# First projections of half 0 taken from x without 1/rms, with a fixed order up to the third feature tile

## The chip, the cores and the metric

The kernel runs on one core of one Trainium2 chip. The metric is the device time of one execution in microseconds. A core has TensorE (PE, with its weight loads shown as PEld), VectorE (DVE), ScalarE (ACT), GpSimd (POOL) and SyncE (SP, which here only issues DMAs). Each works through its own queue in order and waits on semaphores for the others.

## The reference, cut to what matters

One layer with 1024 positions and 1024 features; only its first step is touched by the change:

```python
def rmsnorm(x, g):
    y = x * lax.rsqrt(jnp.mean(x * x, axis=-1, keepdims=True) + EPS)
    return y * g

def swiglu(x, w_gate, w_up, w_down):
    return (jax.nn.silu(x @ w_gate) * (x @ w_up)) @ w_down

x = x + 0.5 * swiglu(rmsnorm(x, ffn1_norm), ffn1_w_gate, ffn1_w_up, ffn1_w_down)
x = x + hybrid_mixer(rmsnorm(x, mix_norm), ...)
x = x + 0.5 * swiglu(rmsnorm(x, ffn2_norm), ffn2_w_gate, ffn2_w_up, ffn2_w_down)
y = rmsnorm(x, final_norm)
```

Each position's row is multiplied by one number, its 1/rms, and each feature by its gain. As 1/rms belongs to a position, it can be put to the rows before a projection or to the projection's products after it.

## The kernel before

**Numbers.** TensorE multiplies in fp32r. To keep fp32 accuracy every operand is split into a high part (a cast on ACT, `S.copy`, L92) and a low part (source minus high part, on DVE, L85 by way of `sub`), and every product is three matmuls of 128 x 128 by 128 x 512: high by high, high by low, low by high (`PASSES`).

**Layout.** x is held with features on partitions, as 8 tiles of 128 features by 1024 positions; a *half* is 512 positions (`xh(k, n)`). The inner dimension of the feed-forward step, 2816, is cut into 22 feature tiles of 128. A product of 1024 features has eight inner steps: `q` is the half of the features (four steps each).

**Order of the work.** Tiles 0 and 1 are taken plainly (`plain`): half 0 of tile 0, half 0 of tile 1, half 1 of tile 0, half 1 of tile 1, with 48 matmuls each (gate and up, two banks of PSUM, 8 inner steps, 3 passes). From tile 2 on (`ups`) a tile's four blocks (gate and up by two halves) are taken together in Strassen's way, with seven products of 12 matmuls, in the order 1, 5, 6, 2, 7, 3, 4 (`UPS`), each of a left operand made from the weights (L11, T1, T2, L12, T3, L22, T4) and a right one made from x (R11, S1, S2, R21, S3, S4, R22). R11 and R21 are half 0, R12 and R22 half 1; S1 to S4 are sums and differences of these. After each second tile, `down` takes the pair through the down projection, 84 matmuls (L588).

**The start.** `Norm.add` squares a feature tile on ACT (L300) and adds it to a chain (L88) on the engine `chain`; `Norm.fin` sums over partitions with a tiny matmul (L318), takes the power -0.5 on POOL (L329), puts it on a diagonal (L333), spreads it over the partitions with another matmul (L337) and, if `keep`, copies it to SBUF (L341). `Norm.raw` (L345) makes x times gain times 1/rms on DVE. `half0` makes R11 and R21, `half1` makes R12, R22, S1 and S2 and POOL's subtractions (L85, hraw) for S3 and S4, `half1_end` S3 and S4. Half 0's chain is on DVE, half 1's on POOL. Half 0's 1/rms is left in PSUM, half 1's is copied to SBUF.

**Weights and queues.** `plan` and `plan_plain` put loads and splits in a list of steps; `pump` takes steps from its head as long as buffers are free, and `tick` calls it, counts planned time and resumes the generators given to `spawn`. All loads go through SP's queue. `pre` makes the operands of a pair's down projection.

**What fixes the order.** `in_order` chains all instructions of an engine in the order of the program; `behind` only puts later instructions behind the last one of that chain. Before, the order of TensorE, DVE, ACT and POOL is fixed up to the end of `half0`; after that TensorE alone is, and a scheduler places the others.

Of the kernel before, what the change touches and what calls it, by code (L numbers as in the profile page):

```python
# [16 lines left out]
P = 128  # L17
# [38 lines left out]
def trunk(ctx: ExitStack, tc: tile.TileContext, a, out):  # L56
# [22 lines left out]
    def t2(name):  # L79
        return room("t2", name)  # L80
# [36 lines left out]
    def pump(n=None):  # L117
        while todo and n != 0:
            n = n and n - 1
            tag, step = todo[0]  # L120
            if not tag():
                return
            todo.popleft()
            step()

    def free(tag, n=1):
        used[tag] -= n
        assert used[tag] >= 0
# [42 lines left out]
            if p == 6:  # L171
                sums(4)

    def load(st, src):
        def go(i):
            st[i] = room("wr", "raw")
            nc.sync.dma_start(out=st[i], in_=src[i])

        for i in range(2):
            todo.append((room_for("wr"), lambda i=i: go(i)))  # L180

    def plan_plain(key, src, order, home=None, when=None):
# [18 lines left out]
        load(st, src)  # L201
# [40 lines left out]
    def spawn(gen, wait=0.0):  # L242
        later.append([clock[0] + wait, gen])

    def tick(us):
        pump()
        clock[0] += us
        for e in list(later):
            if e[0] <= clock[0]:
                w = next(e[1], None)  # L250
                if w is None:
                    later.remove(e)
                else:
                    e[0] = clock[0] + w
# [9 lines left out]
    S.activation(warm, nhalf[:, 0:1], AF.Silu)  # L264
    ones = cp.tile([P, P], F32, name="ones")
    V.memset(ones, 1.0)
    ident = cp.tile([P, P], F32, name="ident")
# [4 lines left out]
    def xh(k, n):  # L272
        return xs[k][:, n * HALF:(n + 1) * HALF]
# [15 lines left out]
    class Norm:  # L289


        def __init__(self, c, w=HALF, chain=None):
            self.c, self.w, self.n, self.chain, self.sums = c, w, w // P, chain, []

        def x(self, k):
            return xs[k][:, self.c:self.c + self.w]

        def square(self, k):
            q = t2("sq")[:, :self.w]
            S.activation(q, self.x(k), AF.Square, scale=D ** -0.5)  # L300
            return q

# [17 lines left out]
        def fin(self, bank, keep=True, waits=(2.7, 1.3), fill=lambda: None):  # L320

            n = self.n
            st = bank("st")
            self.stat([st[:, 2 * j:2 * j + 2] for j in range(n)], self.sums[0], True, True)
            ss = tiny.tile([P, 8], F32, tag="st", name=nm("ss"))
            fill()
            V.tensor_scalar_add(ss[:, 0:2 * n], st[:, 0:2 * n], EPS)
            r = tiny.tile([P, 4], F32, tag="rs", name=nm("rs"))
            G.tensor_tensor(r[:, :n], ss.rearrange("p (j c) -> p j c", c=2)[:, :n, 0], nhalf[:, :n], op=ALU.pow)  # L329
            fill()  # L330
            yield waits[0]
            dg = t2("dg")[:, :self.w]
            V.tensor_tensor(dg.rearrange("p (j c) -> p j c", j=n), ident.unsqueeze(1).to_broadcast([P, n, P]),  # L333
                            r[:, :n].unsqueeze(2).to_broadcast([P, n, P]), op=ALU.mult)
            yield waits[1]
            rp = bank("rb")[:, :self.w]
            nc.tensor.matmul(rp, ones, dg, start=True, stop=True)  # L337
            self.r = rp
            if keep:
                self.r = t2("rb")[:, :self.w]  # L340
                S.copy(self.r, rp)  # L341
            fill()

# [16 lines left out]
    class Ffn:  # L360
        def __init__(self, i, g):
            self.i, self.g = i, g
            self.raws, self.h, self.acts, self.pool, self.start = {}, {}, {}, None, None


        def weights(self):
            w, wd = a[f"ffn{self.i}_w"], a[f"ffn{self.i}_wd"]
            by_k = ("L11", "L21", "L12", "L22")
            plan_plain((self.i, "f", 0), w[0], by_k)
# [86 lines left out]
        def plain(self):  # L456
            for n in range(2):
                for f in range(2):
                    pss = [self.bank(4 * n + 2 * f + m) for m in range(2)]
                    for q in range(2):  # L460
                        lts = [need(((self.i, "f", f), f"L{m + 1}{q + 1}")) for m in range(2)]
                        for k, rk in enumerate(self.r_of(f"R{q + 1}{n + 1}")):
                            for m in range(2):
                                for t, (i, j) in enumerate(PASSES):
                                    c = 512 * i + k * P
                                    nc.tensor.matmul(pss[m], lts[m][:, c:c + P], rk[j],
                                                     start=(q == 0 and k == 0 and t == 0),
                                                     stop=(q == 1 and k == 3 and t == 2))
# [9 lines left out]
                        tick(1.36)  # L478


        def ups(self, f, pre=None):
# [135 lines left out]

        def run(self, after, shut, ranges):
            since = here()
            self.plain()  # L620
            for _ in self.side:
                pass
            spawn(self.half1_end())
            if self.start:
                behind(self.start)
            for f in range(2, NF):
                g = f // 2 - 1
                if f % 2:
                    self.ups(f)
                else:  # L630
                    self.ups(f, lambda: self.pre(g))
                    self.down(g)
            shut()
            in_order(since, nc.tensor)
            self.end = here()
            self.down_last(after, ranges)
# [421 lines left out]
    side = lambda es, n: es.enter_context(tc.tile_pool(name=n, bufs=1, reuse_waits="tile"))  # L1058

    f1, f2 = Ffn(1, 0), Ffn(2, 2)  # L1060
    n1 = [Norm(0, chain=V), Norm(HALF, chain=G)]
    n2 = [Norm(0), Norm(HALF, chain=G)]
    n3 = [Norm(0), Norm(HALF)]
    tail = [(0, HALF), (HALF, 256), (HALF + 256, 256)]
# [6 lines left out]
    eh, ep = ExitStack(), ExitStack()  # L1071
    f1.pool = side(eh, "h1")
    f1.pp = psum(ep, "p1")
    for k in range(KT):
        nc.sync.dma_start(out=xh(k, 0), in_=a["x"][k * P:(k + 1) * P, 0:HALF])
    nc.sync.dma_start(out=gains, in_=a["gains"])
    nc.sync.dma_start(out=ident, in_=a["ident"])
    pump(2)
    for k in range(KT):
        n1[0].add(k)  # L1080
    begin = n1[0].fin(f1.bank_norm, False)
    next(begin)
    pump(2)
    next(begin)
    next(begin, None)
    pump(4)
    for k in range(KT):
        nc.sync.dma_start(out=xh(k, 1), in_=a["x"][k * P:(k + 1) * P, HALF:T])
    nc.sync.dma_start(out=w_a1, in_=a["w_a1"])
    for k, _ in enumerate(f1.half0(n1[0])):  # L1090
        if k >= 4:
            pump(1)
        n1[1].add(k)
    f1.start = in_order(0, nc.tensor, V, S, G)
# [6 lines left out]
    f1.side = second(f1, n1[1], 8.0)  # L1101
    spawn(f1.side)
    pump()
    hm = [[], []]

    def to_mix(n, d):
# [164 lines left out]
```

## Time and profile before

| | before |
|---|---|
| median of 3 runs | 1818.57 us (1815.8 to 1819.06) |
| the profiled execution's own time | 1820.42 us |
| its span, first to last instruction | 1818.6 us |
| PE busy | 1743.9 us, 96% |
| DVE busy | 1377.7 us, 76% |
| ACT busy | 830.1 us, 46% |
| POOL busy | 649.6 us, 36% |
| granted TensorE clock, mean | 0.981 |

The time of an execution is the span and 1.8 us around it. Busy time is added up over each engine's instructions. Matmuls overlap each other, so a busy TensorE is not one at its peak; the start times of matmuls show its pace. In rows of the timeline an "x8" stands for eight instructions in a row that were merged, with the time from the first's start to the last's end; the bracket names the idle time before them and what ended it.

### The profile page before, as it was taken

How to read it: one execution, taken by the hardware profiler on the slowest of the kernel's cores; microseconds unless marked ns; L12 is line 12 of the kernel's file. 1: busy time of each engine (PE TensorE's matmuls, PEld its weight loads, DVE VectorE, ACT ScalarE, POOL GpSimd, SP SyncE). 2: the span in 40 equal slices, each digit the busy share in tenths (PEclk: the TensorE clock that was granted, in tenths of full speed). 3: DMA queues.
4: the chain of work that ended last, by engine and by line, in shares of the span. 5: the costliest groups of instructions: out<-in, count | busy, mean ns of one | idle time of the engine just before them, and what ended most of it. 6: DMA issues, size and time to landing. Idle time of an engine off the chain costs nothing.

```text
span 1818.6 us, 20907 instructions
## 1 busy us (share of the span) xinstructions
PE 1743.9 (96%) x7774; PEld 1426.4 (78%) x7774; DVE 1377.7 (76%) x1825; ACT 830.1 (46%) x1439; POOL 649.6 (36%) x442
## 2 busy tenths in 40 slices
PE   5999999999999998899999999999999999999994
PEld 4788888888888875788888887888888888888883
DVE  6897778877798775765646668787788777887785
ACT  4445445554455444532352444454455544554443
POOL 3454254533444232220211021442545335442433
PEclk9999999999999998999999999999999999999997
DMA  5011212111111211222122222012121121112102
GB/s 188 24 47 47 70 47 67 49 47 59 58 46 47 70 53 46 70 92 81 62 90 90 82 72 96 21 35 70 47 70 47 46 66 50 47 48 69 58 13 93
DMA packets 35110, 112.92 MB, mean 62 GB/s; under 512 B 4384, under 2 KB 6848, under 8 KB 35008
## 3 DMA queue, kind: packets, MB, share of 16 engines
q1 hardware_dynamic: 33376, 109.48, 18.3%
q10 hardware_dynamic: 1632, 2.10, 0.3%
q8 instruction: 61, 1.00, 0.2%
q14 instruction: 41, 0.34, 0.1%
HBM read 107.37 MB, written 4.19 MB: 61 GB/s over the span
## 4 chain that ended last, share of the span: by engine, by line
PE 47%; issue 21%; POOL 18%; DVE 11%; ACT 2%; DMA 0%; POOLq 0%; SPq 0%; ACTq 0%; DVEq 0%
PE ps L588 16%; POOL x L88 12%; PE pj L702 12%; PE ps L354 5%; PE dn L1007 5%; POOL raw L85 4%; DVE S L85 2%; PE v L757 2%; DVE S L88 2%; POOL hraw L85 2%; PE ps L608 2%; PE sc L826 1%; DVE hraw L345 1%; DVE sq L88 1%; DVE T L85 1%
## 5 line engine op out<-in xcount | busy, mean ns | idle before, releaser
L354 PE MATMUL ps<-R,w 128*128 128x512 f32 x1920 | 455.5, 391 | 8.7 <-DVE act L88 8.6
L354 PEld LDWEIGHTS ps<-R,w 128*128 128x128 f32 x1920 | 359.3, 188 | 91.8 <-DVE act L88 17.1
L588 PE MATMUL ps<-act,w 128*128 128x512 f32 x1680 | 388.1, 391 | 0.0
L588 PEld LDWEIGHTS ps<-act,w 128*128 128x128 f32 x1680 | 313.8, 188 | 71.2 <-DVE act L512 6.5
L354 PE MATMUL ps<-S,w 128*128 128x512 f32 x1440 | 342.0, 391 | 3.0 <-ACT ps L493 3.0
L85 DVE TENSOR_TENSOR w<-raw,w 128x512 fp32r<-128x512 f32 x316 | 278.4, 887 | 77.3 <-ACT w L92 77.3
L354 PEld LDWEIGHTS ps<-S,w 128*128 128x128 f32 x1440 | 271.9, 189 | 60.0 <-ACT ps L493 3.4
L85 POOL TENSOR_TENSOR raw<-raw 128x512 f32<-128x512 f32 x60 | 78.5, 1309 | 612.7 <-DVE w L85 610.9
L92 ACT CAST w<-raw 128x512 fp32r<-128x512 f32 x316 | 195.3, 619 | 173.0 <-POOL raw L85 79.1
L88 POOL TENSOR_TENSOR x<-x,dx 128x512 f32<-128x512 f32 x160 | 266.5, 1702 | 17.3 <-ACT dx L575 17.3
L526 DVE SCALAR_TENSOR_TENSOR x<-ps,x 128x512 f32<-128x512 f32 x320 | 210.2, 683 | 35.5 <-PE ps L588 35.5
L702 PE MATMUL pj<-h,whi 128*128 128x512 f32 x640 | 200.5, 395 | 0.0
L85 DVE TENSOR_TENSOR wlo<-raw,whi 128x1024 fp32r<-128x1024 f32 x64 | 80.4, 1256 | 89.5 <-PE pj L702 47.7
L85 DVE TENSOR_TENSOR w<-T,w 128x512 fp32r<-128x512 f32 x120 | 118.1, 984 | 38.1 <-ACT w L92 38.1
L702 PEld LDWEIGHTS pj<-h,whi 128*128 128x128 f32 x640 | 119.0, 189 | 26.2 <-issue 1.9
L218 ACT CAST whi<-raw 128x1024 fp32r<-128x1024 f32 x64 | 67.0, 1047 | 139.1 <-PE pj L702 81.8
L702 PE MATMUL pj<-h,wlo 128*128 128x512 f32 x320 | 124.9, 390 | 0.0
L85 DVE TENSOR_TENSOR act<-act,act 128x512 fp32r<-128x512 f32 x98 | 105.3, 1076 | 13.6 <-ACT act L92 13.6
L92 ACT CAST w<-T 128x512 fp32r<-128x512 f32 x120 | 74.6, 622 | 54.3 <-PE ps L354 32.0
L85 POOL TENSOR_TENSOR raw<-raw,raw 128x512 f32<-128x512 f32 x60 | 97.3, 1622 | 4.6
L92 ACT CAST act<-act 128x512 fp32r<-128x512 f32 x98 | 60.8, 622 | 74.8 <-PE ps L588 44.2
L85 DVE TENSOR_TENSOR T<-raw,raw 128x512 f32<-128x512 f32 x60 | 48.7, 812 | 55.7 <-POOL raw L85 55.7
(170 smaller groups left out, 2133.3 us busy)
## 6 DMA issues: line engine op xcount, KB each, us to landing
raw<-in_ffn_w SPq DMA_DIRECT2D x88, 512.0 KB, 3.5
raw<-in_ffn_wd SPq DMA_DIRECT2D x44, 512.0 KB, 3.7
raw<-in_w_fm SPq DMA_DIRECT2D x40, 512.0 KB, 3.5
raw<-in_w_out SPq DMA_DIRECT2D x16, 512.0 KB, 3.5
x<-in_x SPq DMA_DIRECT2D x16, 256.0 KB, 6.3
raw<-in_w_v SPq DMA_DIRECT2D x8, 512.0 KB, 3.5
out<-y SPq DMA_DIRECT2D x2, 512.0 KB, 2.9
out<-y ACTq DMA_DIRECT2D x2, 512.0 KB, 2.8
```

The source lines that it names most:

```text
L85: eng.tensor_tensor(o, x, y, op=ALU.subtract)
L88: eng.tensor_tensor(o, x, y, op=ALU.add)
L92: S.copy(hi, src)
L218: S.copy(st[1], st[0])
L345: V.scalar_tensor_tensor(o, self.x(k), gains[:, g, k:k + 1], self.r, op0=ALU.mult, op1=ALU.mult)
L354: nc.tensor.matmul(ps, lt[:, c:c + P], rk[j], start=(start and n == 0), stop=(n == last), skip_group_check=True)
L526: V.scalar_tensor_tensor(xh(d, n), ps, 0.5, xh(d, n), op0=ALU.mult, op1=ALU.add)
L588: nc.tensor.matmul(ps, l2[i], r[0][j], start=(start and n == 0), stop=(n == 2), skip_group_check=True)
L608: nc.tensor.matmul(ps, l2[i], rts[h][q][:, 512 * j + o:512 * j + o + w], start=(q == 0 and k == 0), stop=(q == 1 and k == 2))
L702: nc.tensor.matmul(pss[f], w[i][:, k, f * P:(f + 1) * P], h[j][:, 4 * kh + k, :], start=(kh == 0 and k == 0 and n == 0), stop=(kh == 1 and ...
L757: nc.tensor.matmul(pss[t], h[i][:, kk, t * P:(t + 1) * P], u[j][:, k * 512:(k + 1) * 512], start=(kk == 0 and i == 0 and j == 0), stop=(kk ...
L1007: nc.tensor.matmul(pss[j], w[p][:, f * 512 + j * P:f * 512 + (j + 1) * P], act[q][i][:, f * 512:(f + 1) * 512], start=(i == 0 and f == 0 a ...
```

## The change

For half 0 of tiles 0 and 1 the right operands become x times gain (X11 and X21, split like the rest), with no 1/rms; the products of gate and up are multiplied by 1/rms afterwards, on DVE, ahead of Silu. Weights of tile 0 and the gains are loaded through ACT's queue, x through SP's; x of half 1 is loaded behind tile 1's weights. Half 0's chain of squares goes to POOL, half 1's to DVE. R11 and R21 are still needed from tile 2 on: ACT multiplies by the gain and POOL by 1/rms (`raw0`). The differences of x's halves are formed in another order: POOL takes r0 = raws0 - r0 and r1 = r1 - r0, and S1 = raws0 + r1. All buffers are assigned by hand. The order of TensorE, DVE, ACT and POOL is that of the program up to the end of tile 2's `ups`; `hold` stops `pump` in `tick` until `rest` has been through.

```diff
-            nc.sync.dma_start(out=st[i], in_=src[i])
+            queue.dma_start(out=st[i], in_=src[i])
...
     def tick(us):
-        pump()
+        if not hold:
+            pump()
...
+        def block(self, f, n, rights):
+            pss = [self.bank(4 * n + 2 * f + m) for m in range(2)]
+            for q in range(2):
+                lts = [need(((self.i, "f", f), f"L{m + 1}{q + 1}")) for m in range(2)]
+                for k, rk in enumerate(self.r_of(rights[q])):
+                    for m in range(2):
+                        for t, (i, j) in enumerate(PASSES):
...
+                    yield pss
...
+        def opening(self, n0, n1, load1):
+            T = [t2("op") for _ in range(14)]
...
+            def xpart(k):
+                t, g = h[("X11", "X21")[k // 4]], gains[:, self.g, k:k + 1]
+                S.mul(t[:, 0, k % 4, :], xh(k, 0), g)
+                V.scalar_tensor_tensor(t[:, 1, k % 4, :], xh(k, 0), g, t[:, 0, k % 4, :].bitcast(F32),
+                                       op0=ALU.mult, op1=ALU.subtract)
+
+            def raw0(i):
+                o = raws[divmod(i, 4)]
+                S.mul(o, xh(i, 0), gains[:, self.g, i:i + 1])
+                G.tensor_tensor(o, o, n0.r, op=ALU.mult)
...
+            pump(1)
+            xpart(0)
+            pump(1)
+            xpart(1)
+            for k in range(6):
+                n0.add(k)
+                xpart(k + 2)
+                if k in (1, 2):
+                    pump(1)
+            pump(2)
+            load1()
+            b = self.block(0, 0, ("X11", "X21"))
+            for ps00 in b:
+                pass
+            n0.add(6)
+            n0.add(7)
+            pump(4)
+            for k in range(5):
+                n1.add(k)
+            fin = n0.fin(self.bank_norm)
+            next(fin)
+            pump(2)
+            b = self.block(1, 0, ("X11", "X21"))
+            n1.add(5)
+            next(b), next(b)
+            next(fin)
+            n1.add(6)
+            n1.add(7)
+            next(b)
+            next(fin, None)
+            a00 = T[13]
+            V.tensor_tensor(a00, ps00[0], n0.r, op=ALU.mult)
+            V.tensor_tensor(ps00[1], ps00[1], n0.r, op=ALU.mult)
+            S.activation(a00, a00, AF.Silu)
+            raw0(0)
...
+            b = self.block(0, 1, ("R12", "R22"))
+            a10 = T[12]
+            row(0)
+            for i in range(8):
+                if i < 7:
+                    row(i + 1)
+                rowpart(i)
+                if i == 1:
+                    V.tensor_tensor(a10, ps10[0], n0.r, op=ALU.mult)
+                    V.tensor_tensor(ps10[1], ps10[1], n0.r, op=ALU.mult)
+                    S.activation(a10, a10, AF.Silu)
+                if i == 3:
+                    V.tensor_tensor(a10, a10, ps10[1], op=ALU.mult)
+                if i < 4:
+                    raw0(4 + i)
+                    sub(G, r[0, i], raws[0, i], r[0, i])
+                ps01 = next(b)
+            for _ in b:
+                pass
+            for k in range(4):
+                sub(G, r[1, k], r[1, k], r[0, k])
+            h["S3"] = h["X21"]
+            parts("S3", range(4), lambda k: r[0, k])
...
+            b = self.block(1, 1, ("R12", "R22"))
+            pump(2)
+            V.tensor_tensor(a01, a01, ps01[1], op=ALU.mult)
+            next(b), next(b)
+            parts("R11", range(4), lambda k: raws[0, k])
+            next(b), next(b)
+            h["S1"] = h["X11"]
+            for k in range(4):
+                add(V, raws[0, k], raws[0, k], r[1, k])
+                self.part("S1", k, raws[0, k])
+                if k == 1:
+                    pump(3)
...
+            def rest():
+                pump(1)
+                self.right("S2", "S3")
+                parts("S2", range(4), lambda k: r[1, k])
+                pump(2)
+                parts("R21", range(4), lambda k: raws[1, k])
+                yield 2.7
+                pump(1)
+                h["S4"] = h["R12"]
+                for k in range(4):
+                    sub(G, raws[1, k], raws[1, k], r[1, k])
+                for k in range(4):
+                    parts("S4", (k,), lambda k: raws[1, k])
+                    if k == 1:
+                        yield 2.7
+                raws.clear()
+                hold.clear()
...
-    n1 = [Norm(0, chain=V), Norm(HALF, chain=G)]
+    n1 = [Norm(0, chain=G), Norm(HALF, chain=V)]
```

In `run`, the opening takes the place of `plain` and `half1_end`, and the chain of `in_order` now ends behind `ups` of tile 2:

```diff
-                if f % 2:
+                if f == 2 and self.norms:
+                    self.ups(f, lambda: self.pre(g))
+                    start = in_order(0, nc.tensor, V, S, G)
+                    self.down(g)
+                    behind(start)
+                elif f % 2:
```

## Rows read from the trace of the kernel before

**Rows 1.** The page, busy time by engine and TensorE in 40 slices of the span.

```profile
PE 1743.9 (96%) x7774; PEld 1426.4 (78%) x7774; DVE 1377.7 (76%) x1825; ACT 830.1 (46%) x1439; POOL 649.6 (36%) x442
...
PE   5999999999999998899999999999999999999994
```

**Rows 2.** Timeline of TensorE: start us, length us, engine, line, operation, tiles.

```profile
20.56 10.08 PE L466 MATMUL ps<-R,w 128*128 128x512 f32 x31 [1.49 <-ACT R L92]
...
51.21 5.60 PE L466 MATMUL ps<-S,w 128*128 128x512 f32 x24
...
62.09 5.60 PE L466 MATMUL ps<-S,S 128*128 128x512 f32 x24
67.53 5.60 PE L466 MATMUL ps<-R,S 128*128 128x512 f32 x24
72.97 5.60 PE L354 MATMUL ps<-R,w 128*128 128x512 f32 x24
81.54 5.49 PE L354 MATMUL ps<-S,w 128*128 128x512 f32 x12 [2.96 <-ACT ps L493]
...
98.49 19.51 PE L588 MATMUL ps<-act,w 128*128 128x512 f32 x84
117.84 5.60 PE L354 MATMUL ps<-R,w 128*128 128x512 f32 x24
...
153.81 3.06 PE L354 MATMUL ps<-R,w 128*128 128x512 f32 x12 [0.45 <-DVE act L88]
```

**Rows 3.** Timeline and windows of the start: loads, first casts, DMA (last columns: share, GB/s).

```profile
0.72 1.28 ACT L264 ACT_TABLE_LOAD   x1 [0.72 <-PEq L1263]
7.27 2.38 SPq L177 DMA_DIRECT2D raw<-in_ffn_w  x4
12.18 2.42 ACT L92 CAST w<-raw 128x512 fp32r<-128x512 f32 x4 [0.86 <-DMA raw<-in_ffn_w]
...
0.00:5.38 5.38, 0.00 (x0) 0.00 (x0) 0.22 (x2) 2.74 (x4) 0.19 (x4) 1.00 0.58 171
5.38:20.56 15.18, 3.94 (x10) 2.28 (x11) 9.54 (x16) 6.72 (x12) 1.39 (x1) 1.00 0.99 365
```

**Rows 4.** Timeline: the sums over partitions and the spread of the second norm.

```profile
35.45 1.06 PE L318 MATMUL ps<-ones,sq 128*128 128x2 f32 x8 [0.31 <-POOL sq L88]
42.16 1.02 PE L337 MATMUL ps<-dg,ones 128*128 128x512 f32 x2
```

**Rows 5.** Timeline of DVE and POOL, each alone and both at work.

```profile
31.81 1.29 POOL L88 TENSOR_TENSOR sq<-sq,sq 128x512 f32<-128x512 f32 x1 [1.35 <-ACT sq L300]
44.51 4.72 DVE L345 SCALAR_TENSOR_TENSOR hraw<-x,gains,rb 128x512 f32<-128x512 f32 x7
51.55 2.50 DVE L85 TENSOR_TENSOR R<-hraw,R 128x512 fp32r<-128x512 f32 x4
60.15 4.69 POOL L85 TENSOR_TENSOR hraw<-hraw,hraw 128x512 f32<-128x512 f32 x1 [19.40 <-DVE hraw L85]
66.50 1.75 POOL L85 TENSOR_TENSOR hraw<-hraw,hraw 128x512 f32<-128x512 f32 x1
67.01 1.78 DVE L85 TENSOR_TENSOR w<-raw,w 128x512 fp32r<-128x512 f32 x1
68.21 3.44 POOL L85 TENSOR_TENSOR hraw<-hraw,hraw 128x512 f32<-128x512 f32 x2
68.72 3.48 DVE L85 TENSOR_TENSOR S<-hraw,S 128x512 fp32r<-128x512 f32 x2
1121.02 1.79 DVE L345 SCALAR_TENSOR_TENSOR hraw<-x,gains,rb 128x512 f32<-128x512 f32 x1
```

**Rows 6.** Windows: length, then busy (count) of PE, PEld, DVE, ACT, POOL; PEclk, DMA, GB/s.

```profile
51.20:72.97 21.77, 21.77 (x97) 18.02 (x96) 21.77 (x28) 8.62 (x16) 12.82 (x6) 1.00 0.08 25
72.97:98.49 25.52, 22.44 (x85) 17.66 (x84) 19.83 (x24) 10.88 (x20) 9.77 (x7) 0.87 0.07 21
81.50:86.80 5.30, 5.26 (x12) 4.12 (x13) 2.41 (x5) 1.53 (x3) 0.00 (x0) 0.50 0.32 99
```

More of the change, by code (lines that the diff above doesn't have):

```diff
@@ L172, in plan, with load, plan_plain @@
                 sums(4)
-    def load(st, src):
+    def load(st, src, queue=nc.sync):
         def go(i):
             st[i] = room("wr", "raw")
-            nc.sync.dma_start(out=st[i], in_=src[i])
+            queue.dma_start(out=st[i], in_=src[i])
         for i in range(2):
             todo.append((room_for("wr"), lambda i=i: go(i)))
-    def plan_plain(key, src, order, home=None, when=None):
+    def plan_plain(key, src, order, home=None, when=None, queue=nc.sync):
         st = {}
@@ L199, in part @@
             todo.append((when or room_for("wo"), go))
-        load(st, src)
+        load(st, src, queue)
         where = {"L11": (0, 0), "L12": (1, 1), "L21": (0, 1), "L22": (1, 0)}
@@ L243, in spawn @@
         later.append([clock[0] + wait, gen])
+    hold = []
     def tick(us):
-        pump()
+        if not hold:
+            pump()
         clock[0] += us
@@ L263, in trunk @@
     warm = cp.tile([P, 1], F32, name="warm")
-    S.activation(warm, nhalf[:, 0:1], AF.Silu)
     ones = cp.tile([P, P], F32, name="ones")
@@ L293, in __init__, with room @@
             self.c, self.w, self.n, self.chain, self.sums = c, w, w // P, chain, []
+            self.homes = {}
+        def room(self, s):
+            return self.homes[s] if s in self.homes else t2(s)[:, :self.w]
         def x(self, k):
@@ L298, in square @@
         def square(self, k):
-            q = t2("sq")[:, :self.w]
+            q = self.room(f"sq{k}" if self.homes else "sq")
             S.activation(q, self.x(k), AF.Square, scale=D ** -0.5)
@@ L331, in fin @@
             yield waits[0]
-            dg = t2("dg")[:, :self.w]
+            dg = self.room("dg")
             V.tensor_tensor(dg.rearrange("p (j c) -> p j c", j=n), ident.unsqueeze(1).to_broadcast([P, n, P]),
@@ L339, in fin @@
             if keep:
-                self.r = t2("rb")[:, :self.w]
+                self.r = self.room("rb")
                 S.copy(self.r, rp)
@@ L362, in __init__ @@
             self.i, self.g = i, g
-            self.raws, self.h, self.acts, self.pool, self.start = {}, {}, {}, None, None
+            self.raws, self.h, self.acts, self.pool, self.norms = {}, {}, {}, None, None
         def weights(self):
@@ L368, in weights @@
             by_k = ("L11", "L21", "L12", "L22")
-            plan_plain((self.i, "f", 0), w[0], by_k)
+            plan_plain((self.i, "f", 0), w[0], by_k, queue=nc.scalar if self.i == 1 else nc.sync)
             plan_plain((self.i, "f", 1), w[1], by_k, lambda: self.place("S3", [P, 4, 1024]), lambda: self.pool is not None)
@@ L478, in plain @@
                         tick(1.36)
+        def block(self, f, n, rights):
[5 more added lines that the diff above has]
+                        for t, (i, j) in enumerate(PASSES):
+                            c = 512 * i + k * P
+                            nc.tensor.matmul(pss[m], lts[m][:, c:c + P], rk[j],
+                                             start=(q == 0 and k == 0 and t == 0),
+                                             stop=(q == 1 and k == 3 and t == 2))
+                    yield pss
+                if n and f == 0:
+                    free("wo", 2)
@@ new lines, in opening, with parts, row, rowpart @@
+        def opening(self, n0, n1, load1):
+            T = [t2("op") for _ in range(14)]
+            h, raws, r = self.h, self.raws, {}
+            h["X11"], h["X21"] = self.place("S2"), self.place("S4")
+            for n, norm in enumerate((n0, n1)):
+                t = hp.tile([P, 2, 4, HALF], F32, tag="h", name=nm("sq"))
+                norm.homes.update({f"sq{k}": t[:, k // 4, k % 4, :] for k in range(KT)}, dg=T[0], rb=T[1 + n])
+            for s in ("R12", "R22", "R11", "R21"):
+                self.right(s, "R")
+            for q, k in ((0, 0), (0, 2), (1, 0)):
+                t = room("ao", "hraw")
+                raws[q, k], raws[q, k + 1] = t[:, 0:512], t[:, 512:1024]
+            raws[1, 2], raws[1, 3] = T[4], T[5]
+            for k in range(4):
+                r[0, k], r[1, k] = T[(3, 11, 10, 0)[k]], T[6 + k]
+            def xpart(k):
[7 more added lines that the diff above has]
+                G.tensor_tensor(o, o, n0.r, op=ALU.mult)
+            def parts(s, ks, src):
+                for k in ks:
+                    self.part(s, k, src(k))
+            pump(1)
[33 more added lines that the diff above has]
+            raw0(0)
+            next(b)
+            fin = n1.fin(self.bank_norm)
+            next(fin)
+            V.tensor_tensor(a00, a00, ps00[1], op=ALU.mult)
+            raw0(1)
+            next(b), next(b)
+            next(fin)
+            raw0(2)
+            raw0(3)
+            next(b)
+            next(fin, None)
+            ps10 = next(b)
+            for _ in b:
+                pass
+            def row(i):
+                n1.raw(r[divmod(i, 4)], self.g, i)
+            def rowpart(i):
+                self.part(("R12", "R22")[i // 4], i % 4, r[divmod(i, 4)])
+            b = self.block(0, 1, ("R12", "R22"))
[15 more added lines that the diff above has]
+                ps01 = next(b)
+            for _ in b:
+                pass
+            for k in range(4):
+                sub(G, r[1, k], r[1, k], r[0, k])
+            h["S3"] = h["X21"]
+            parts("S3", range(4), lambda k: r[0, k])
+            a01, a11 = T[11], T[10]
+            S.activation(a01, ps01[0], AF.Silu)
+            b = self.block(1, 1, ("R12", "R22"))
[3 more added lines that the diff above has]
+            parts("R11", range(4), lambda k: raws[0, k])
+            next(b), next(b)
+            h["S1"] = h["X11"]
[4 more added lines that the diff above has]
+                    pump(3)
+            for ps11 in b:
+                pass
+            S.activation(a11, ps11[0], AF.Silu)
+            V.tensor_tensor(a11, a11, ps11[1], op=ALU.mult)
+            self.acts[0], self.acts[1] = (a00, a01), (a10, a11)
+            def rest():
[9 more added lines that the diff above has]
+                    sub(G, raws[1, k], raws[1, k], r[1, k])
+                for k in range(4):
+                    parts("S4", (k,), lambda k: raws[1, k])
[3 more added lines that the diff above has]
+                hold.clear()
+            hold.append(1)
+            spawn(rest())
@@ L619, in run @@
             since = here()
[L620 to L625, printed above, removed]
+            if self.norms:
+                self.opening(*self.norms)
+            else:
+                self.plain()
+                for _ in self.side:
+                    pass
+                spawn(self.half1_end())
             for f in range(2, NF):
                 g = f // 2 - 1
-                if f % 2:
+                if f == 2 and self.norms:
[4 more added lines that the diff above has]
+                elif f % 2:
                     self.ups(f)
@@ L1073, in trunk, with load_x, load1 @@
     f1.pp = psum(ep, "p1")
[L1074 to L1077, printed above, removed]
-    pump(2)
[L1079 to L1094, printed above, removed]
+    def load_x(n):
+        for k in range(KT):
+            nc.sync.dma_start(out=xh(k, n), in_=a["x"][k * P:(k + 1) * P, n * HALF:(n + 1) * HALF])
+    def load1():
+        nc.sync.dma_start(out=ident, in_=a["ident"])
+        load_x(1)
+        nc.sync.dma_start(out=w_a1, in_=a["w_a1"])
+    nc.scalar.dma_start(out=gains, in_=a["gains"])
+    pump(2)
+    load_x(0)
+    S.activation(warm, nhalf[:, 0:1], AF.Silu)
+    f1.norms = (*n1, load1)
     def second(f, norm, wait):
@@ L1099, in second @@
         yield from f.half1(norm)
-    f1.side = second(f1, n1[1], 8.0)
-    spawn(f1.side)
-    pump()
     hm = [[], []]
```

## The prediction

> **What bounds the kernel now.** I read the page first: TensorE is busy 96% of the span, no other engine is near it, and the slices show one thin slice, the first [rows 1]. The timeline of TensorE then shows two regimes. From 98.49 us on, the first product of the down projection, feature tiles follow each other at one pitch: 84 matmuls start at 98.49 and the next group starts at 117.84, 0.23 us each [rows 2]. The groups of 24 from 51.21 to 67.53 (three between these starts) give the pitch exactly, (67.53 - 51.21) / 72 = 0.2267 us [rows 2]. Before 98.49 it is not so: the first projection matmul starts at 20.56, and the 192 + 84 matmuls of tiles 0, 1 and 2 would take 276 x 0.2267 = 62.6 us but take 77.9. So 20.6 us are lost ahead of the first matmul and 15.4 after it (about 2 of these are the sums of the second norm, which are work). The change touches only this stretch; what it is worth is how far it moves the instant 98.49, since nothing later waits long enough to give a shift back. I call that instant E.
>
> **The early start (removed: the wait for 1/rms).** Before, the first weight is cast at 12.18 and the first part of R11 is there at 20.56 [rows 2, 3]. After, the first product needs only a weight and x times its gain. The weights now go through ACT's queue beside SP's x. By 5.38 the DMA had moved 171 GB/s x 5.38 = 0.92 MB, then 365 GB/s [rows 3]. If the queues take turns, the first 0.5 MB of weights lands with about 0.75 MB of x, at 5.38 + 0.33/365 GB/s = 6.3; if x goes first, as before, at 12.18. I take 7.0, near the lower end because only the first x is ahead in line. A cast (2.42 / 4 = 0.60) and a subtraction of 0.69 later, TensorE starts at 8.3. Loading Silu's table (1.28) and issuing three DMAs on ACT (2.38 / 4 = 0.60 each) lie before 7.0 [rows 3] and cost nothing; with that cover gone they would cost 3.1 us.
>
> **Half 0 of tile 0.** ACT has 4 weight casts, 8 parts and 6 squares here, 18 x 0.60 = 10.8 us, so it ends ahead of TensorE: the first 31 matmuls took 10.08 us before, at the low pitch with which TensorE begins [rows 2], then 17 x 0.2267 = 3.9, so 8.3 + 14.0 = 22.3. POOL's new chain of 7 adds, at 1.70 (see below) from 10.9 on, ends at 22.8, and the sums' matmuls wait for it. **Half 0 of tile 1:** 48 x 0.2267 = 10.9, with two groups of sums at 1.06 and two spreads at 1.02 [rows 4], 22.8 + 15.1 = 37.9. Before, these 96 matmuls were done at 51.21 [rows 2]. Here 13.3 us are won. The product with 1/rms is three DVE operations a tile that read PSUM, beside TensorE, and cost nothing while DVE has slack; the squares, the gains' multiplications on ACT and SP's reordered loads (x of half 1 behind tile 1's weights) have slack too, at least 5 us each.
>
> **Where it goes: DVE against POOL.** POOL had little to do in this stretch before: 7 adds, 8 subtractions and a few more. The change puts there 8 multiplications of raw0 (before, DVE made these parts in one operation that read 1/rms from PSUM), and 4 + 4 + 4 subtractions. While POOL was at work, from 65 to 77, both engines slowed: POOL's operations follow at 68.21 - 66.50 = 1.71, DVE's at 68.72 - 67.01 = 1.71, strictly by turns, where DVE alone has 2.50 / 4 = 0.62 and POOL alone 1.29 [rows 5]. A pair costs 0.60 for DVE and 1.10 for POOL. DVE's operations with PSUM in them are free of it; rows made with 1/rms from SBUF are not: one took 1.79 with POOL busy, against 4.72 / 7 = 0.67 [rows 5]. The Trainium skill (SBUF — State Buffer, section "SBUF: two separate sides") calls this an exclusive lock that the first holds for the whole instruction. By that a pair would cost 1.29 + 0.69 = 1.98 and the sum below, with 18 such pairs, some 5 us more; no row here shows more than 1.71, so the rows stand.
>
> **Half 1 of tile 0.** It can start when the second 1/rms has been copied, at 37.2. In a fixed order DVE makes 8 rows (0.67) and 8 low parts (0.60), 10.2 us; POOL makes in between 4 multiplications, 4 subtractions of r0 and 3 of r1, 11 x 1.10 = 12.1. ACT's copies fit beside. So the last part is there at 37.2 + 22.3 = 59.5, and TensorE ends at 60.5, against 10.9 us of matmuls. Before, the same 144 matmuls were done at 62.09 [rows 2]: 1.6 us are left of the 13.3. Bounds: nothing of POOL in the way (TensorE's 10.9) and the 1.98 per pair.
>
> **Half 1 of tile 1, and tile 2.** Half 1 of tile 1 finds its operands: 60.5 + 10.9 = 71.4; product 1 of tile 2 ends at 74.1. DVE meanwhile, from 59.5: S3 (4), a weight, R11 (4), 9 x 0.60, an act 0.6, two POOL operations 2.2, so 67.7. Then S1 in strict order: an add 0.69, ACT's copy 0.62, a subtraction 0.69, four times, 8.0, with a sum and a weight 1.2 and one POOL operation 1.1: 78.0. Product 5, last quarter, ends at 78.7; before, 72.97 + 5.44 = 78.4 [rows 2]. Even. Up to weight L22 DVE then has T2, S2 (4), a sum, L12, R21 (4), T3, S4 (4), 5 operations of pre() and L22 itself: 22 x 0.60 = 13.2, and POOL 4 subtractions for S4 and one of pre(), 5.5. So L22 is there at 96.7. TensorE has done products 6, 2 and 7 by about 89 and waits; products 3 and 4 are 5.44, and after so long a wait they start slow: before, after 2.96 us of waiting, 12 matmuls ran at a granted clock of 0.50 (its 1.2 GHz level) and took 5.3 instead of 2.7 [rows 2, 6], 2.6 more. E = 96.7 + 5.4 + 2.6 = 104.7, that is 6.2 us later than 98.49. Before, DVE was as full only from 51 to 73 (21.77 of 21.77), then had 5.7 us of idle time [rows 6]; it is DVE and POOL together that set the end now.
>
> **Against the clock.** The profiled execution took 1820.42 us, its span 1818.6; the median of the runs is 1818.57. +6.2 gives 1826.6 for the former and 1824.8 for the median, which I forecast. About 0.2% (3.6 us) can be told from no change; the runs of before lie 3.3 us apart.
>
> **Rivals.** (a) *Faster: DVE keeps POOL out.* At 60.15 a POOL operation needed 4.69 us because seven DVE operations passed at 0.60 [rows 5]. If DVE passes like this in half 1 of tile 0, that half takes TensorE's 10.9 plus about 1.5, half 1 of tile 1 ends near 61 and tile 2 at 80; POOL's 20 operations of 1.27 come in DVE's gaps, end late and hold S4 by some 8 us: E = 88, 1808. It is decided where each low part waits for ACT's copy: a gap there lets POOL in. Against it: from 64.8 to 76.7 POOL came in every time. (b) *No change:* half of the 18 POOL operations that I count fall into DVE's own waits for ACT or beside those that read PSUM, -10; tile 2 is then held by the S1 chain instead, which gives some 5 back: E near 99.5, 1819.6. (c) *The clock falls in half 1 of tile 0 and before product 5 too*, as TensorE is half idle there: twice 2.6 more, 1830. For: it fell after a wait of 2.96 us; against: a wait of 0.45 us ahead of a product left it at 3.06 us, near the usual 2.88 [rows 2]. (d) *It does not start earlier:* the weights land at 12.18 as before, because x and weights share the same DMA, which was 99% busy from 5.38 to 20.56 [rows 3]; 5.2 us later throughout, 1830.
>
> **How the numbers follow.** Forecast 0.32, (a) 0.22, (b) 0.26, (c) 0.12, (d) 0.08. The forecast's own range, by the bounds of the first landing (-1 to +5) and of the pairs (0 to +5), is 1820 to 1831. Over all cases 1807 to 1832: it takes in (c), (d) and most of (a), and leaves out about 1 in 10 below and less above. Faster by over 0.2% (under 1814.9): (a) and a little of (b), 0.24. Slower (over 1822.2): most of the forecast, (c) and (d), 0.50. Within: 0.26.
>
> **What would show it.** In the timeline after: first L11 cast near 7; 96 matmuls done near 38; in half 1 of tile 0 DVE and POOL by turns at 1.7, TensorE at about 22 us for 48 matmuls; product 3 of tile 2 waiting for DVE's L22 with a half clock behind; first down product near 105. Wrong, if TensorE runs that half in 11 to 13 us, or if the first down product starts before 95.

## The result, and the profile after

The change makes the kernel slower: 1832.17 us (1831.83 to 1832.86, 4 runs) against 1818.02, a ratio of 1.0082 with a 95% interval of 1.0068 to 1.0095. The profiled execution took 1832.21 us, its span 1830.4, against 1818.6: 11.8 us more, which lie in the first 130 us. I had forecast slower, by 6.2 us, which is less than half of the 14.2 measured; the time lies just past the end of the range, and the runs bear out one of the two reasons given.

The page after, busy time by engine and TensorE's slices, answers to [rows 1]:

```profile
PE 1746.5 (95%) x7774; PEld 1423.9 (78%) x7774; DVE 1387.4 (76%) x1825; ACT 838.1 (46%) x1456; POOL 666.1 (36%) x454
...
PE   7789999999999998899999999999999999999994
```

The first slice is fuller (7 for 5), as planned, but the second and third, which were full, are not (7 and 8 for 9). TensorE's timeline, against [rows 2], shows when:

```profile
7.87 10.58 PE L496 MATMUL ps<-S,w 128*128 128x512 f32 x31 [7.87 <-ACT S L521]
...
24.08 0.95 PE L324 MATMUL ps<-ones,sq 128*128 128x2 f32 x8
...
42.15 0.50 PE L496 MATMUL ps<-R,w 128*128 128x512 f32 x1 [1.02 <-ACT R L92]
...
64.10 11.04 PE L496 MATMUL ps<-R,S 128*128 128x512 f32 x48
74.98 2.88 PE L360 MATMUL ps<-R,w 128*128 128x512 f32 x12
77.70 2.41 PE L360 MATMUL ps<-S,w 128*128 128x512 f32 x9
...
86.17 0.39 PE L360 MATMUL ps<-R,w 128*128 128x512 f32 x1
...
92.98 4.46 PE L360 MATMUL ps<-S,w 128*128 128x512 f32 x12 [3.06 <-ACT ps L675]
100.83 1.22 PE L360 MATMUL ps<-R,w 128*128 128x512 f32 x2 [3.38 <-ACT w L92]
102.77 4.20 PE L360 MATMUL ps<-R,w 128*128 128x512 f32 x10 [0.71 <-DVE w L85]
108.43 3.00 PE L360 MATMUL ps<-R,w 128*128 128x512 f32 x12 [1.47 <-DVE act L88]
111.27 13.99 PE L763 MATMUL ps<-act,w 128*128 128x512 f32 x61
...
130.31 2.88 PE L360 MATMUL ps<-R,w 128*128 128x512 f32 x12
```

The first projection matmul starts at 7.87 instead of 20.56. Half 1 of tile 0 begins at 42.15 (before, 51.21), a lead of 9 us. That half then takes 22 us instead of 10.9, and at 64.10 the change is 2 us behind (62.09). Tile 2 adds the rest: products 5 and 6 come in pieces and take 8.5 us (77.70 to 86.17) for 24 matmuls of 5.4, product 7 waits 3.1 us, product 3 3.4 us, product 4 1.5 us. The first down product starts at 111.27 (98.49) and tile 3 at 130.31 (117.84), 12.5 later; of this 0.7 us comes back by the end.

Both losses can be read in the windows (columns as in [rows 6]) of half 1 of tile 0 and of the end of tile 2:

```profile
42.10:64.10 22.00, 13.35 (x48) 8.65 (x49) 21.42 (x20) 9.19 (x16) 19.12 (x12) 1.00 0.00 0
...
86.20:111.30 25.10, 15.93 (x50) 11.10 (x49) 20.65 (x26) 10.00 (x19) 14.06 (x8) 0.80 0.12 42
```

In the first window DVE is busy 21.42 of 22.00 us with 20 operations, 1.07 each, and POOL 19.12 with 12. The timeline of both there shows the turns of [rows 5]:

```profile
53.43 1.71 POOL L528 TENSOR_TENSOR op<-op,op 128x512 f32<-128x512 f32 x1
53.94 1.74 DVE L85 TENSOR_TENSOR R<-op,R 128x512 fp32r<-128x512 f32 x1
55.10 1.74 POOL L85 TENSOR_TENSOR op<-hraw,op 128x512 f32<-128x512 f32 x1
55.61 1.77 DVE L351 SCALAR_TENSOR_TENSOR op<-x,gains,op 128x512 f32<-128x512 f32 x1
56.80 1.71 POOL L85 TENSOR_TENSOR op<-op,op 128x512 f32<-128x512 f32 x1
57.31 1.74 DVE L85 TENSOR_TENSOR R<-op,R 128x512 fp32r<-128x512 f32 x1
```

DVE's operations start 1.67 and 1.70 us apart, and each part of TensorE's right operand needs two of them: 3.4 us for six matmuls that take 1.36. In tile 2 the loss is another one. The timeline of POOL, ACT and DVE around products 7, 3 and 4:

```profile
87.12 4.68 POOL L85 TENSOR_TENSOR hraw<-hraw,op 128x512 f32<-128x512 f32 x2 [16.69 <-DVE R L85]
...
90.61 0.62 ACT L92 CAST R<-hraw 128x512 fp32r<-128x512 f32 x1 [2.83 <-POOL hraw L85]
...
92.35 0.58 ACT L675 COPY ps<-ps 128x512 f32<-128x512 f32 x1
...
99.16 0.62 ACT L92 CAST act<-S 128x512 fp32r<-128x512 f32 x1 [2.30 <-DVE S L85]
...
100.17 0.61 ACT L92 CAST w<-raw 128x512 fp32r<-128x512 f32 x1
...
107.61 0.68 DVE L88 TENSOR_TENSOR act<-ps,p 128x512 f32<-128x512 f32 x1
```

Product 7 needs ACT's copy of product 6's bank (L675), product 3 the cast of L22 at 100.17, product 4 the add at 107.61, which makes u1, one of the two results of tile 2 (u0 is the other) that the down projection takes. Each is short; each stands in its engine's fixed order behind something that waits and that TensorE does not need yet: the copy behind casts for S4, which wait for POOL; L22 behind an operand of the down projection, which waits for DVE; the add behind the next weights.

### The profile page after: what moved, and what is told of

It is laid out like the page before. It is cut to its first block, busy times and chain, and to the rows that moved or that the text cites. A ratio compares the mean times of both kernels' runs of the same rounds, so it can differ in the third digit from the quotient of the medians.

```text
span 1830.4 us, 20949 instructions
## 1 busy us (share of the span) xinstructions
PE 1746.5 (95%) x7774; PEld 1423.9 (78%) x7774; DVE 1387.4 (76%) x1825; ACT 838.1 (46%) x1456; POOL 666.1 (36%) x454
## 4 chain that ended last, share of the span: by engine, by line
PE 46%; issue 21%; POOL 18%; DVE 12%; ACT 3%; DMA 0%; POOLq 0%; ACTq 0%; DVEq 0%
PE ps L763 16%; POOL x L88 12%; PE pj L883 11%; PE ps L360 5%; PE dn L1188 5%; POOL raw L85 4%; DVE S L85 2%; PE v L938 2%; DVE S L88 2%; PE ps L783 2%; PE sc L1007 1%; DVE w L85 1%; POOL hraw L85 1%; DVE R L85 1%; DVE T L85 1%
```

## The experiments

Two theories: the port (DVE and POOL block each other, so the new work on POOL is paid by DVE too), and the order (ready operations stand behind waiting ones). A third, that DVE alone has too many operations, is the rival of both. In each expectation theory A is the one that its edit tries, and B or "rival" stands against it. All kernels start from the changed one. In the table "first down" is the start of the down projection's first matmul and "tile 3" that of tile 3's first product, from TensorE's timeline.

| | half 1 of tile 0, us | first down | tile 3 | span |
|---|---|---|---|---|
| before | 10.9 | 98.49 | 117.84 | 1818.6 |
| changed | 22.0 | 111.27 | 130.31 | 1830.4 |
| e1 tile 2 left to the scheduler | 22.0 | 112.20 | 131.28 | 1832.3 |
| e2 rows from PSUM | 17.3 | 107.04 | 126.08 | 1826.8 |
| e3 POOL's work moved back | 13.0 | 113.96 | 133.00 | 1831.5 |
| e4 S4 on DVE | 22.0 | 108.52 | 127.56 | 1827.9 |
| e5 raw0 and rows from PSUM | 15.6 | 104.79 | 123.83 | 1824.0 |
| e6 order of tile 2 | 22.0 | 108.27 | 127.73 | 1826.0 |
| e7 e5 and e6 | 15.6 | 101.25 | 120.31 | 1817.8 |
| e8 e6 and hold | 22.0 | 103.03 | 123.00 | 1823.6 |
| e9 e5 and e8 | 15.6 | 93.70 | 117.78 | 1816.8 |
| e10 e9, sums earlier | 15.6 | 92.53 | 116.57 | 1815.4 |
| e11 e10, pre() later | 15.6 | 88.67 | 113.84 | 1812.1 |

Each row is one execution. The spread of the first norm, which lies ahead of the edits of e1 to e9, starts at 30.62 in the changed kernel and between 30.13 (e4) and 30.78 (e8) in the others, so half a microsecond between two rows says nothing. The spans say less: the times of the kernel before, taken beside these, lie between 1814.33 and 1820.62.

**e1, tile 2 left to the scheduler.**

```diff
-                    self.ups(f, lambda: self.pre(g))
                     start = in_order(0, nc.tensor, V, S, G)
+                    self.ups(f, lambda: self.pre(g))
```

> The changed kernel with one edit: the fixed order of DVE, ACT and POOL ends ahead of tile 2's products instead of behind them, so that the scheduler places the operations of tile 2. Theory A (in the written order operations that are ready stand behind ones that wait: ACT's copies behind those fed by POOL, weight L22 behind pre()): the first down product, at 111.3 us in the changed kernel, comes back to 100 to 103, product 7 no longer waits 3 us and product 3 no longer 3.4; span 1820 to 1823. Theory B (DVE and POOL together have more work than the stretch holds, whatever the order): the first down product stays at 107 or later and the span at 1826 or more. Both: half 1 of tile 0 still takes 22 us.

Theory A failed in this form: 112.20. Product 7 no longer waits for the copy, though it starts no earlier (93.29), because product 6 waited twice for DVE's parts of S2, ahead of which the scheduler had put other operations, and product 2 started at 90.00 instead of 86.17; the first two of POOL's subtractions for S4 took 7.73 us together, and product 3 came in pieces:

```profile
89.46 7.73 POOL L85 TENSOR_TENSOR hraw<-hraw,op 128x512 f32<-128x512 f32 x2 [4.24 <-DVE R L85]
...
102.85 0.96 PE L360 MATMUL ps<-R,w 128*128 128x512 f32 x3 [2.40 <-DVE R L85]
```

So a fixed order is not the fault as such; the scheduler's was no better.

**e2, rows from PSUM.**

```diff
-            fin = n1.fin(self.bank_norm)
+            fin = n1.fin(self.bank_norm, False)
```

> The changed kernel with one edit: half 1's 1/rms stays in PSUM, so the eight rows of half 1 read x from SBUF and 1/rms from PSUM. Theory A (DVE operations with two SBUF inputs take turns with POOL's): rows run beside POOL, half 1 of tile 0 falls from 22 us to 15 to 18, rows last 0.75 us instead of 1.77 there, and the first down product comes 3 to 6 us earlier than 111.3. Rival (POOL's chain or ACT's copies pace that half, not the turns): it stays at 21 to 22 us.

As theory A says, on all counts: 17.3 us for the half, 4.2 us earlier at the first down product (0.4 of it ahead of the edit). The line's instructions (minimum, median, maximum ns), first in the changed kernel, then here:

```profile
L351 DVE SCALAR_TENSOR_TENSOR op<-x,gains,op x8: 734/880/1775, 40.4 to 59.0; 128x512 f32<-128x512 f32 x8
```

```profile
L351 DVE SCALAR_TENSOR_TENSOR op<-x,gains,ps x8: 730/735/747, 39.4 to 53.4; 128x512 f32<-128x512 f32 x8
```

The same operation on the same data, its second operand in PSUM instead of SBUF, no longer waits for POOL.

**e3, POOL's work moved back.**

```diff
-                if i < 4:
-                    raw0(4 + i)
-                    sub(G, r[0, i], raws[0, i], r[0, i])
                 ps01 = next(b)
             for _ in b:
                 pass
+            for i in range(4):
+                raw0(4 + i)
+                sub(G, r[0, i], raws[0, i], r[0, i])
```

> The changed kernel with one edit: POOL's four multiplications of raw0 and its four subtractions of r0 come behind the eight parts of half 1 of tile 0 instead of between them. Theory A (the turns with POOL cost that half its 11 us): the half takes 11 to 14 us instead of 22, its DVE operations 0.6 to 0.7 us each. But S3 to S1 then wait for POOL, so product 5 or 6 waits: the first down product between 105 and 112. Rival (ACT or DVE alone paces the half): 18 us or more for the half.

The half takes 13.0 us: what paced it was POOL. But all that is won comes back, with 2.7 us on top, because S3 and, behind it, R11 and S1 now wait for the same POOL operations (product 1 waits 2.9 us). The work has to go, not to move.

**e4, S4 on DVE.**

```diff
-                    sub(G, raws[1, k], raws[1, k], r[1, k])
+                    sub(V, raws[1, k], raws[1, k], r[1, k])
```

> The changed kernel with one edit: the four subtractions for S4 are on DVE instead of POOL. Theory A (ACT's copy of product 6's bank stands in ACT's queue behind copies of S4 that wait for POOL, which DVE keeps out): product 7 starts at 89 to 90 instead of 93.0 and at full clock, products 3 and 4 come 3 to 5 us earlier, the first down product at 106 to 108. Theory B (DVE is simply full there): DVE's four extra operations of 0.6 leave the first down product at 110 to 113.

2.75 us are won, 0.5 of them ahead of the edit, and 108.52 lies just past theory A's 106 to 108: product 7 runs near full pace (3.04 us), but starts at 91.39, not at 89 to 90, as it still waits 1.9 us for the copy, ahead of which ACT now has S4's casts waiting 2.3 us for DVE.

**e5, raw0 and rows from PSUM; e6, order of tile 2; e7, both.** For e5 half 1's 1/rms goes to bank 0 and stays there, and all of raw0 is made while DVE waits for that norm:

```diff
-                S.mul(o, xh(i, 0), gains[:, self.g, i:i + 1])
-                G.tensor_tensor(o, o, n0.r, op=ALU.mult)
+                V.scalar_tensor_tensor(o, xh(i, 0), gains[:, self.g, i:i + 1], n0.p, op0=ALU.mult, op1=ALU.mult)
```

Here `n0.p` is the spread 1/rms in its bank. For e6, beside e4's edit, the adds for S1 come ahead of its splits, S4's splits a product later, and L22 and T4 ahead of `pre`:

```diff
+            for k in range(4):
                 add(V, raws[0, k], raws[0, k], r[1, k])
...
-                for k in range(4):
-                    parts("S4", (k,), lambda k: raws[1, k])
-                    if k == 1:
-                        yield 2.7
+                yield 2.7
+                parts("S4", range(4), lambda k: raws[1, k])
+                pump(2)
```

> The changed kernel with POOL's multiplications taken away, not moved: raw0 is made by DVE in one operation that reads 1/rms from PSUM (as before the change), in the stretch where DVE waits for half 1's norm, and half 1's 1/rms is left in PSUM too (in bank 0), so its rows read PSUM. Theory A (what the change lost is the port that DVE and POOL share, and it was lost to the 8 multiplications and the rows with two SBUF inputs): half 1 of tile 0 takes 12 to 15 us instead of 22, and the first down product comes at 99 to 104 instead of 111.3; span 1818 to 1823. Theory B (DVE's own count of operations is the limit): DVE has 8 operations more, 5 us, so the first down product stays at 107 or later.

> The changed kernel with tile 2's order alone edited: the four adds for S1 ahead of its splits, S4's subtractions on DVE, S4's splits behind product 6's copy, weights L22 and T4 ahead of pre(). Theory A (a part of the loss is waits in a fixed order, each behind something that is not needed): the first down product at 101 to 105, against 108.5 with S4's subtractions on DVE alone; product 7 without a wait, product 3 without the 3.4 us. Theory B (the port or DVE is full there): 107 or later. Half 1 of tile 0 keeps its 22 us in both.

> Both edits together. If the losses are two separate ones, of the port in half 1 of tile 0 and of the order in tile 2, they add up: the first down product at 90 to 96, ahead of the 98.5 of the kernel before, span 1810 to 1816, a ratio of 0.996 to 0.999 to the kernel before. If DVE's count is the limit, it comes no earlier than the better of the two alone, 100 or later, and the ratio is 1.000 or more.

e5 is theory A's, a little less than it said (15.6 us for the half, 104.79). DVE has eight operations more than in the changed kernel and yet everything comes 6.5 us earlier. These eight alone do not settle the rival, DVE's own count, since they lie ahead of half 1, where DVE had waited; inside that half DVE is busy for all of the 15.60 us. It falls by e3, where DVE does the half's rows and parts in 13.0 us, and by e4, where it has four operations more in tile 2 and the first down product comes earlier. e6 and e7 read like theory B by their figures, but TensorE's timeline, here of e6, says otherwise:

```profile
86.59 2.88 PE L360 MATMUL ps<-S,w 128*128 128x512 f32 x12
89.96 0.73 PE L360 MATMUL ps<-R,w 128*128 128x512 f32 x2 [0.48 <-ACT w L92]
91.80 4.15 PE L360 MATMUL ps<-R,w 128*128 128x512 f32 x10 [1.10 <-DVE w L85]
103.01 5.46 PE L360 MATMUL ps<-R,w 128*128 128x512 f32 x12 [7.07 <-DVE act L88]
```

Product 7 lost its wait and product 3 most of it, and products 5 and 6 run without a gap (product 2 starts at 83.11); product 4 got a wait of 7.1 us, and then ran slow. Its add stood behind the first weights of the down projection, one of which waits for POOL, as it had in the changed kernel, where most of that wait was hidden behind product 3's. e7 missed its figures: 1821.15 us in the median of ten runs against 1816.82 for the kernel before beside it, a ratio of 1.0023 (1.0013 to 1.0033) where 0.996 to 0.999 was expected; the execution in the table is one of its fastest.

**e8 and e9, the hold.**

```diff
                 raws.clear()
+                yield 2.7
+                yield 2.7
                 hold.clear()
+                pump()
```

> Tile 2's order alone once more (half 1 of tile 0 as in the changed kernel), with the weights of the first down projection held back until product 7 has been issued: before, DVE's add for act u1, which product 4 waits for, stood behind those weights and behind POOL's sum of them, and product 4 waited 7 us. If the fixed order of tile 2 is a loss of its own beside the port: the first down product at 99 to 102 instead of 108.3, with half 1 of tile 0 still at 22 us, span 1817 to 1820. If DVE is full: 105 or later.

> The same hold put to both edits (raw0 and rows from PSUM, tile 2's order). The two losses add: the first down product at 92 to 96 instead of 101.3, span 1809 to 1813, under the kernel before. If DVE's count is the limit: 99 or later.

e8 moves the first down product by 5.2 us, 1 us short of what was expected, and the span less (1823.6 for 1817 to 1820); e9's first down product is where it was expected, its span is not (1816.8 for 1809 to 1813), because the down projection then waited at its seventh matmul for act u0, again behind those weights:

```profile
93.70 1.52 PE L765 MATMUL ps<-act,w 128*128 128x512 f32 x6
98.34 19.60 PE L765 MATMUL ps<-act,w 128*128 128x512 f32 x78 [3.11 <-DVE act L689]
```

So tile 3's start is the better mark. By it the port edit alone (e5) wins 6.5 us, the edit of tile 2 alone (e8) 7.3, both together (e9) 12.5: two losses, nearly added up. The 7.3 is not all order: e8 holds e4's edit, which takes S4 off POOL and by itself wins 2.75, so order and hold are worth about 4.6.

**e10 and e11, the same two ideas further.** e10 takes `n0.fin`'s first step ahead of half 1's squares, and five of these behind its second; e11 calls `pre` behind product 7 and holds the weights one product longer.

```diff
+            fin = n0.fin(self.bank_norm)
+            next(fin)
-            for k in range(5):
+            for k in range(3):
                 n1.add(k)
-            fin = n0.fin(self.bank_norm)
-            next(fin)
             pump(2)
             b = self.block(1, 0, ("X11", "X21"))
-            n1.add(5)
             next(b), next(b)
             next(fin)
-            n1.add(6)
-            n1.add(7)
+            for k in range(3, 8):
+                n1.add(k)
```

```diff
-                if p == 6 and pre:
+                if p == (7 if f == 2 and self.norms else 6) and pre:
                     pre()
```

> As the run before, and half 0's sums taken ahead of half 1's chain on DVE: in the changed kernel the spread of 1/rms waited 1.4 us for DVE, whose first operation on the sums stood behind the splits of tile 1's weights and four adds. If that order costs what the trace shows, all later steps move 1 to 2 us ahead: the first down product at 90.5 to 94.5, ratio to the kernel before 0.994 to 0.998. If DVE is full from there on, the gain is taken back before the first down product and it stays where the run before has it.

> As the run before (both edits, early sums), with two more steps of the same kind: pre()'s operands come behind DVE's add for act u1 instead of ahead of it, and the weights of the first down projection behind the two DVE operations of product 3. In the run before, product 4 waited 1.9 us for u1 and the seventh matmul of the down projection 3.1 us for act u0, each behind these. If such waits in a fixed order are losses that add up, tile 3 starts at 112 to 114.5 instead of 116.57 (117.84 in the kernel before), ratio to the kernel before 0.996 to 0.9985. If DVE's count is the limit by now, the weights or operands that went back are the next to be late, and tile 3 starts at 115.5 or later.

e10 gives 0.9986 (0.9977 to 0.9995), its ratio just outside the expected 0.994 to 0.998, e11 0.9975 (0.9964 to 0.9985) as expected: 1814.01 us against 1819.74 in the same sitting. This is faster than both kernels. What is left of the waits in e11:

```profile
83.55 5.29 PE L360 MATMUL ps<-R,w 128*128 128x512 f32 x22 [1.11 <-DVE w L85]
88.67 0.64 PE L765 MATMUL ps<-act,w 128*128 128x512 f32 x2
91.19 2.84 PE L765 MATMUL ps<-act,w 128*128 128x512 f32 x7 [1.88 <-DVE w L85]
95.00 19.00 PE L765 MATMUL ps<-act,w 128*128 128x512 f32 x75 [0.97 <-ACT sg L693]
```

## Why the prediction was right in sign, short in size and wrong about tile 2

**The early start** was right: the first cast at 6.57 (7.0 taken, 6.3 to 12.18 as bounds), the first matmul at 7.87 (8.3). Rival (d) falls with it.

**Half 0** failed by 3.2 us: the copy of the second 1/rms, for which half 1 waits, is done at 40.4 (39.80 and 0.59) instead of 37.2. The step charged the turns with POOL's new chain of squares to POOL alone, at 1.70 an operation, and held that DVE's products with 1/rms "cost nothing while DVE has slack". DVE had none at the places that count. While POOL adds its squares, each low part of x takes DVE 1.7 us (0.75 before POOL began), and half 0 of tile 0 ends at 24.2 instead of 22.3:

```profile
14.05 8.17 POOL L88 TENSOR_TENSOR sq<-sq 128x512 f32<-128x512 f32 x5 [0.34 <-ACT sq L306]
17.59 5.18 DVE L522 SCALAR_TENSOR_TENSOR S<-x,gains,S 128x512 fp32r<-128x512 f32 x3
19.41 4.83 PE L496 MATMUL ps<-S,w 128*128 128x512 f32 x17 [0.96 <-DVE S L522]
```

The timeline of DVE and TensorE around the first norm shows the next part:

```profile
22.69 2.48 DVE L85 TENSOR_TENSOR S<-raw,S 128x512 fp32r<-128x512 f32 x4
25.10 3.07 DVE L88 TENSOR_TENSOR sq<-sq 128x512 f32<-128x512 f32 x4
28.08 0.16 DVE L333 TENSOR_SCALAR ss<-ps 128x8 f32<-128x8 f32 x1
30.62 1.13 PE L343 MATMUL ps<-op,ones 128*128 128x512 f32 x2 [1.36 <-DVE op L339]
```

The sums are there at 25.03; DVE takes them at 28.08, behind four splits and four adds that stand earlier in its order. The spread waits 1.36 us and that of the second norm 0.56. e10 mended the order around the norm and won 1.2 us; no run takes the chain of squares off POOL, so what the turns of half 0 cost is read from the timeline alone.

**Half 1 of tile 0** was right in mechanism and size: from the copy of 1/rms to TensorE's end 23.3 us were predicted (37.2 to 60.5) and 23.7 measured (40.4 to 64.1); e2, e3 and e5 show that it is POOL's operations and the rows' second SBUF operand that make it so. The pair of 1.70 held. The Trainium skill (SBUF — State Buffer, section "SBUF: two separate sides") would have the second wait out the whole instruction of the first, which with this case's 1.29 and 0.69 makes an estimate of 1.98 a pair. The six rows in the section on the result show 1.67 to 1.70. That section names DVE operations with two SBUF inputs among those that the lock concerns, and with this the rows and e2 agree.

**Tile 2** failed by another 3 us: 104.7 was predicted and 111.27 measured, of which 3.6 stood at the end of half 1 (64.10 for 60.5). The step counted operations of DVE and POOL up to L22 and let TensorE finish products 6, 2 and 7 "by about 89". The chain for S1, an add, a copy and a subtraction four times over, held product 5 as the step has it, and the gaps in products 5 and 6 come from there; e6, with the adds ahead, has none. The step left out that ACT's order is fixed too: product 7 waited for a copy behind S4's casts and ended at 97.4, L22's cast stood behind an operand of `pre`, and product 4 waited for an add behind the next weights. That product 3 would wait for L22 with a slow clock behind came true, but not because DVE was full: of the 25.1 us shown above it was busy for 20.65, and in e8, with four operations more on DVE and half 1 as it was, the last ten matmuls of product 3 start at 91.99 instead of 102.77. By tile 3's start e8 wins 7.3 us, 2.75 of them by taking S4 off POOL (e4) and the rest by order and hold. The slow clock behind a wait, which I charged once with 2.6, came twice: product 7 took 4.46 us and product 3's last ten matmuls 4.20, and the granted clock was 0.65 over the one (92.9 to 97.5) and 0.55 over the other (100.8 to 107.0), between its levels of 1.2 and 2.4 GHz.

**The sign** was in part luck. By the sum the change was still 1.6 us ahead at the end of half 1, so that "slower" rested on the count of tile 2 alone; measured, it was 2.0 behind there. With tile 2's losses mended (e8) it is still slower, tile 3 starting at 123.00 (117.84). **The range** of 1820 to 1831 does not follow from the bounds that it names: these, added to 1824.8, give about 1824 to 1835.

**The rivals.** (a) DVE did keep POOL out, at 87.12 (4.68 us for two), but that cost time, since S4 waited for POOL; in half 1, where I had placed it, the two took turns. (b) POOL's operations did not fall into DVE's waits. (c) The clock did not fall in half 1 (1.00 granted) nor ahead of product 5, but behind products 2 and 7. The spans differ by 11.8 us and the medians by 14.2, since the profiled execution of before, at 1820.42, lies 2.4 above the median of its runs; a sum made against that execution cannot see this.

## What to carry to other kernels

Before work is given to GpSimd because it is idle, count how many VectorE operations with two SBUF operands run beside it: in half 1 of tile 0 each of its operations cost VectorE about 1.1 us, and taking the operand from PSUM, or one fused operation on VectorE, was cheaper than the help. An order written by hand has to be checked engine by engine for what stands ahead of each operation that TensorE waits for; a wait that is mended only shows the next one, so the mark to measure by is the start of the next undisturbed stage, not the wait itself. A start that is moved forward is worth only as much as the engines behind it can keep up with.

## What the runs showed of the hardware that was not expected

With the same instructions at the same pace in half 1 of tile 0 the granted clock was 1.00 over that stretch in the changed kernel and 0.84 in e1 and e4; six matmuls took 1.64 to 1.67 us in the one and up to 2.93 in the other, and it changed nothing, since TensorE waited for its operands anyway. The rows of e1:

```profile
52.38 2.93 PE L496 MATMUL ps<-R,w 128*128 128x512 f32 x6 [1.38 <-DVE R L85]
...
42.10:64.10 22.00, 15.44 (x48) 9.88 (x49) 21.41 (x20) 9.20 (x16) 19.11 (x12) 0.84 0.00 0
```

VectorE's back-to-back operations held off two GpSimd operations of 1.3 us, which took 7.73 us together in e1. The first of them took about 6.5, since ACT's cast of its result starts at 95.99; in [rows 5] one needed 4.69.
